# Attention results kept with features on partitions, their norms as rows over DRAM

## The chip, the cores and the metric

One NeuronCore of a Trainium2 chip runs the whole program. The metric is the device time of one execution in microseconds (us); a lower time is better. The engines are TensorE (PE, with its weight loads PEld), VectorE (DVE), ScalarE (ACT), GpSimd (POOL) and SyncE (SP). DMA transfers are issued from the queues of SP, ACT and POOL.

## What is computed

One layer of a hybrid decoder block in float32 on 512 tokens and 1024 features: 16 heads of 64 features, 4 of them MoBA (heads 0 to 3), 6 dilated (heads 4 to 9), 6 FoX (heads 10 to 15). The part that the change touches is what stands between a head's softmax and the output projection:

```python
hn = rms_norm(x, norm_g)
proj = hn @ w_in                      # q, k, v, f_logit, g_fox
...
p = softmax(logits);  o = p @ v       # per head, (tokens, 64)
...
y_moba = rms_norm(to_bsd(o_moba), out_gain[:W_MOBA])
y_fox = rms_norm(to_bsd(o_fox), ...) * sigmoid(g_fox)
y_dil = rms_norm(to_bsd(o_dil), ...)
x = x + concat([y_moba, y_fox, y_dil]) @ w_out
x = x + square(relu(rms_norm(x, mlp_norm) @ w_up)) @ w_down
```

`rms_norm` divides a token's features by the root of their mean square, so each group of heads needs one number per token, and each head's softmax one denominator per token.

## The kernel before

Every float32 product is made of three products of the type fp32r: each operand is split into a high and a low part, and hi·hi, hi·lo and lo·hi are added in PSUM. Weights are split as they stream in: ACT casts the high part (`whi`, L118), DVE subtracts it (`wlo`, L119).

There are three stages. The input projection (`product`, L274) runs over nine chunks of columns (q and k of four heads, then v of four heads, four times, then the FoX gate) and eight blocks of 128 input features. Attention's steps are put between its products by a planner that runs when the program is written: a list `steps`, each with what it needs and a lag after it (`LAG`), a running clock and a price for each step (`COST`), and `attend`, which puts the next eligible step after each triple of products. So PE's order is written out by hand. The other engines' orders come from a scheduler that takes the operations in the order in which it thinks their inputs are there. Each engine runs its own list strictly in order. The output projection follows, in two chunks of columns, each in two parts: part 0 over the MoBA and FoX features that are ready, part 1 over the rest, each part added into the residual by DVE (`out_done`, L748). Then comes the MLP (L876 up, L917 down), which the change leaves alone.

A head's way: `stack_step` transposes q and k and swaps their parts between partitions by DMA (`stk`), and loads the head's bias tile on POOL's queue (`alibi`, L485, for heads 0 to 9; `ck`, L479, rows of a cumulated sum in DRAM copied to 128 partitions, for heads 10 to 15; two buffers each). `s_step` makes four blocks of scores (L516), their maximum (DVE, `mn`, L528) and exponentials (ACT, `p`, L530). `pt_step` transposes p (L543) and splits it (`pth` ACT L549, `ptl` DVE L550). `av_step` (L567) multiplies by v. Its weight is v's high and low parts side by side, so the result `ot` has the 64 features of the one part on partitions 0 to 63 and of the other on 64 to 127; ACT copies it out (`ots`, L572).

`o_step` then adds the two parts: four fp32 transposes on PE (L582) put tokens on partitions, a DVE reduction adds the halves (`osum`, L584), and POOL multiplies by the reciprocal of the denominator into `o_grp` (L591). After a group's last head, `group_norm` squares and adds on ACT (L607), takes the root on DVE (`rsqrt`, L284 to L290) and scales on DVE (L618, or L614 together with the gate for FoX). `y_transpose` (L624) brings features back to partitions for the output projection, split by ACT (L627) and DVE (L628). There are 16 o steps of four transposes, and 32 transposes of y.

PSUM has eight banks: four ("m") for attention and the MLP's first half, four ("acc") for the projections.

Of the kernel before, what the change touches and what calls it, by code (L numbers as in the profile page):

```python
# [156 lines left out]
def hymba_block(ctx: ExitStack, tc: tile.TileContext, a, out):  # L157
# [397 lines left out]
    def av_step(h, half):  # L555
        def f():
# [8 lines left out]
            for j, p in blocks:  # L565
                v = vst[h // 4, j][:, h % 4].rearrange("p a d -> p (a d)")
# [34 lines left out]
    def group_norm(g):  # L601
        o = o_grp[g]
        n = o.shape[2]
        ss = small.tile([P, NT], F32, name="oss")
        for t in range(NT):
            junk = att.tile([P, S], F32, name="ots")[:, :n]
            nc.scalar.activation(junk, o[:, t], AF.Square, accum_out=ss[:, t : t + 1])  # L607
        v = small.tile([P, NT], F32, name="ov")
        r = small.tile([P, NT], F32, name="orr")
        nc.vector.tensor_scalar(v, ss, 1.0 / n, EPS, op0=ALU.mult, op1=ALU.add)  # L610
# [416 lines left out]
```

## Time and profile before

| what | us |
|---|---|
| median of 3 runs | 636.34 (636.05 to 636.53) |
| the profiled execution | 636.59 |
| its span in the trace | 634.8 |
| PE busy | 625.1 (98%) |
| DVE busy | 459.6 (72%) |
| ACT busy | 322.6 (51%) |
| POOL busy | 43.9 (7%) |

PE's busy time is nearly the span, and the granted clock is 0.997 of full speed. Busy time on PE is counted from each matmul's start to its modelled end, and these overlap. What a matmul costs is therefore read from start to start. DVE is busy 72% over the whole, but this mean hides stretches between 124 and 208 us in which it is near 90%.

### The profile page before, as it was taken

The numbers are of one execution on the slowest core, as the hardware profiler recorded it, in microseconds if no ns is written. First come the engines' busy times: TensorE is split into PE (matmuls) and PEld (weight loads), VectorE is DVE, ScalarE is ACT, GpSimd is POOL, SyncE is SP. The second block draws the span as 40 slices with busy tenths as digits, with TensorE's granted clock in tenths as the row PEclk, the third lists the DMA queues.
The fourth block names the chain that finished last, engine by engine and source line by source line (L and its number), as shares of the span: only waits on it lengthen the run. The fifth ranks groups of instructions, "written<-read, shape, count | busy, mean of one in ns | idle before, by whom it ended". The sixth has DMA issues, their size and how long they took to land.

```text
span 634.8 us, 9834 instructions
## 1 busy us (share of the span) xinstructions
PE 625.1 (98%) x3800; PEld 556.0 (88%) x3800; DVE 459.6 (72%) x786; ACT 322.6 (51%) x575; POOL 43.9 (7%) x63
## 2 busy tenths in 40 slices
PE   7999999999999999999999999999999999999997
PEld 6798898898889998888889989898989899989986
DVE  6794695796578666578899766687588766865972
ACT  7457666677777585639553433343334333434320
POOL 4010220121120000001100000000000000000000
PEclk8999999999999999999999999999999999999999
DMA  8534423423522335256624243232530433212213
GB/s 311 160 103 132 125 74 77 131 79 112 138 59 76 101 102 174 74 178 204 133 66 147 71 148 100 83 109 75 167 96 8 163 100 131 68 35 67 68 41 126
DMA packets 24911, 70.03 MB, mean 110 GB/s; under 512 B 3210, under 2 KB 4762, under 8 KB 24864
## 3 DMA queue, kind: packets, MB, share of 16 engines
q1 hardware_dynamic: 18224, 57.84, 28.6%
q10 hardware_dynamic: 4432, 5.77, 3.7%
q0 software_dynamic: 2208, 5.79, 3.7%
q8 instruction: 30, 0.49, 0.3%
q14 instruction: 17, 0.14, 0.1%
HBM read 61.51 MB, written 2.11 MB: 100 GB/s over the span
## 4 chain that ended last, share of the span: by engine, by line
PE 76%; DVE 7%; ACT 1%; issue 1%; DMA 1%; ACTq 0%; POOL 0%; DVEq 0%
PE acc L917 28%; PE m L876 22%; PE acc L274 19%; PE m L516 2%; PE m L567 2%; PE m L543 1%; DVE ptl L550 1%; PE m L497 1%; DMA stk<-stk 1%; DVE qkss L402 1%; DVE wlo L119 1%; DVE qks L420 1%; DVE m L528 1%; DVE qkraw L415 1%; DVE qkv L403 1%
## 5 line engine op out<-in xcount | busy, mean ns | idle before, releaser
L118 ACT CAST whi<-wraw 128x1024 fp32r<-128x1024 f32 (+3 forms) x66 | 66.8, 1015 | 86.5 <-PE acc L917 38.7
L274 PE MATMUL acc<-whi,xh 128*128 128x512 f32 (+3 forms) x284 | 103.5, 364 | 0.7 <-DVE fl L438 0.4
L917 PE MATMUL acc<-hh,whi 128*128 128x512 f32 x256 | 100.2, 391 | 0.0
L917 PE MATMUL acc<-hh,wlo 128*128 128x512 f32 x256 | 99.9, 390 | 0.0
L917 PE MATMUL acc<-hl,whi 128*128 128x512 f32 x256 | 99.6, 389 | 0.0
L119 DVE TENSOR_TENSOR wlo<-wraw,whi 128x1024 fp32r<-128x1024 f32 (+3 forms) x66 | 78.9, 1197 | 28.4 <-ACT whi L118 28.0
L274 PE MATMUL acc<-wlo,xh 128*128 128x512 f32 (+3 forms) x284 | 95.7, 337 | 0.7 <-DVE wlo L119 0.6
L274 PE MATMUL acc<-whi,xl 128*128 128x512 f32 (+3 forms) x284 | 95.8, 337 | 0.0
L876 PE MATMUL m<-zh,whi 128*128 128x256 f32 x224 | 62.8, 280 | 0.0
L876 PE MATMUL m<-zh,wlo 128*128 128x256 f32 x224 | 62.6, 279 | 0.0
L876 PE MATMUL m<-zl,whi 128*128 128x256 f32 x224 | 62.5, 279 | 0.0
L274 PEld LDWEIGHTS acc<-whi,xl 128*128 128x128 f32 x284 | 53.6, 189 | 5.2
L917 PEld LDWEIGHTS acc<-hh,wlo 128*128 128x128 f32 x256 | 48.0, 188 | 10.6 <-DVE wlo L119 0.5
L274 PEld LDWEIGHTS acc<-wlo,xh 128*128 128x128 f32 x284 | 54.0, 190 | 3.7 <-DVE wlo L119 1.5
L274 PEld LDWEIGHTS acc<-whi,xh 128*128 128x128 f32 x284 | 53.7, 189 | 3.7 <-DVE vs L432 0.7
L917 PEld LDWEIGHTS acc<-hl,whi 128*128 128x128 f32 x256 | 48.1, 188 | 9.2 <-issue 0.2
L917 PEld LDWEIGHTS acc<-hh,whi 128*128 128x128 f32 x256 | 48.1, 188 | 9.1 <-issue 0.2
L118 ACT CAST whi<-wsum 128x1024 fp32r<-128x1024 f32 x28 | 29.4, 1049 | 40.2 <-PE m L876 37.6
L926 DVE TENSOR_TENSOR x<-acc,x 128x512 f32<-128x512 f32 (+1 forms) x65 | 42.2, 678 | 9.5 <-PE acc L917 9.4
L119 DVE TENSOR_TENSOR wlo<-wsum,whi 128x1024 fp32r<-128x1024 f32 x28 | 34.3, 1223 | 19.3 <-ACT whi L118 19.3
L530 ACT ACTIVATE p<-m,mn 128x128 f32<-128x128 f32 (+1 forms) x64 | 33.6, 527 | 24.9 <-DVE mn L528 22.8
L876 PEld LDWEIGHTS m<-zh,whi 128*128 128x128 f32 x224 | 42.0, 188 | 1.1
(193 smaller groups left out, 1324.1 us busy)
## 6 DMA issues: line engine op xcount, KB each, us to landing
wraw<-in_w_down SPq DMA_DIRECT2D x32, 512.0 KB, 3.6
ublk<-in_w_up SPq DMA_DIRECT2D x28, 512.0 KB, 3.4
wraw<-in_w_in SPq DMA_DIRECT2D x21, 512.0 KB, 3.8
stk<-stk ACTq DMA_DIRECT2D x32, 128.0 KB, 2.4
wraw<-in_w_out SPq DMA_DIRECT2D x6, 512.0 KB, 4.0
alibi<-in_alibi POOLq DMA_DIRECT2D x10, 256.0 KB, 3.2
x<-in_xT SPq DMA_DIRECT2D x4, 512.0 KB, 5.1
wraw<-in_w_up SPq DMA_DIRECT2D x4, 512.0 KB, 5.4
```

The costliest lines, as they stand in the source:

```text
L118: nc.scalar.copy(hi, raw)
L119: nc.vector.tensor_tensor(lo, raw, hi.bitcast(F32), op=ALU.subtract)
L274: nc.tensor.matmul(dst, lhsT=lhs, rhs=rhs, start=(k == 0 and m == 0), stop=(k == n - 1 and m == 2))
L402: nc.vector.tensor_reduce(ss, sq.rearrange("p (h d) -> p h d", d=DH), axis=AX.X, op=ALU.add)
L403: nc.vector.tensor_scalar(state["v"][:, t], ss, 1.0 / DH, eax[:, t : t + 1], op0=ALU.mult, op1=ALU.add)
L415: nc.vector.tensor_tensor(raw, raw, state["y"][:, t].unsqueeze(2).broadcast_to([P, 8, DH]), op=ALU.mult)
L516: nc.tensor.matmul(ps[:, :n], lhsT=st[0][:, i * P : (i + 1) * P], rhs=st[m][:, :n], start=(m == 1), stop=(m == 2 and h < FOX0),)
L530: nc.scalar.activation(p, ps[:, :n], AF.Exp, bias=mn, scale=-1.0, accum_out=st["den"][:, i : i + 1])
L567: nc.tensor.matmul(ot[:, j * P :], lhsT=v, rhs=p, start=(half == 0 and j == 0), stop=(half == 1 and j == 3))
L876: nc.tensor.matmul(acc[:, f * HALF : (f + 1) * HALF], lhsT=lhs, rhs=rhs, start=first and (f, j, m) == (0, 0, 0), stop=(f, j, m) == (1, 3, ...
L917: nc.tensor.matmul(acc, lhsT=lhs, rhs=rhs, start=(p, k, m) == (0, 0, 0), stop=(p, k, m) == (1, 1, 2))
L926: nc.vector.tensor_tensor(dst[:, cols], acc[:, cols], dst[:, cols], op=ALU.add)
```

## The change

The result of a head stays as `av_step` leaves it, features on partitions. The new code for that is `result`, which takes the place of `o_step`, and `norm_step`, which takes the place of `group_norm`; `y_transpose` becomes `y_parts` without PE.

- The two halves of `ots` are added by a DMA that accumulates, issued on POOL's queue (64 partitions of 2 KB, L617).
- The reciprocal denominators, four columns on 128 partitions, are written to a row in DRAM (`row_to_dram`, 512 pieces of 4 bytes, L351) and read back as 64 copies of that row (`row_copies`, L356), both on POOL's queue. DVE multiplies the sum by the rows (L618). POOL's multiplication L591 goes.
- v's parts are laid out by parity of the head, so that an odd head's sum lands on partitions 64 to 127; its two operations for each tile become four (L450, L451).
- A pair's squares are made by ACT and added by DVE (L628) into a tile that takes a buffer of `ck` (group 0) or of `alibi` (groups 1 and 2). Four matmuls with one column (L636) add them over the partitions; the root goes over DRAM to rows on 128 partitions.
- Groups 0 and 1 are multiplied by these rows (DVE, L650). FoX's are multiplied onto the products: in part 1 of the output projection DVE multiplies each PSUM bank by the row (L785) ahead of the residual's addition (L786).
- The gate chunk of the input projection is turned round: 72 products of 512 columns in place of 96 of 384; DVE multiplies by x's row (in place of ACT's L466), and again into the FoX result (L659).
- The planner's lag "norm" goes from 9 to 10, and the steps "o" and "y" have no price any more.

```diff
+    def row_to_dram(src, name):
+        d = dram.tile([1, S], F32, name=name)
+        nc.gpsimd.dma_start(d.rearrange("o (t p) -> p (o t)", p=P), src)
+        return d
+    def row_copies(dst, d):
+        nc.gpsimd.dma_start(dst, bass.AP(tensor=d.tensor, offset=d.offset, ap=[[0, dst.shape[0]], [1, S]]))
...
+        rows_d["x"] = row_to_dram(rx, "rx_d")
...
-    o_grp = [att.tile([P, NT, (h1 - h0) * DH], F32, name=f"o{g}", bufs=1) for g, (h0, h1, _) in enumerate(GROUPS)]
-    gsig = att.tile([P, NT, NFOX * DH], F32, name="gsig", bufs=1)
+    o_grp = [att.tile([P, (h1 - h0) // 2, S], F32, name=f"o{g}", bufs=1) for g, (h0, h1, _) in enumerate(GROUPS)]
+    gsig = att.tile([P, NFOX // 2, S], F32, name="gsig", bufs=1)
...
+    def gate_operands(k, f, wh, wl):
+        wh, wl = wh[:, f * P : (f + 1) * P], wl[:, f * P : (f + 1) * P]
+        return ((wh, xh[:, k]), (wh, xl[:, k]), (wl, xh[:, k])), lambda acc: acc
...
-            v = att.tile([P, 4, 2, DH], F32R, name="vs", bufs=8)
-            av = acc[:, :256].rearrange("p (h d) -> p h d", d=DH)
-            nc.scalar.activation(v[:, :, 0], av, AF.Copy, scale=rx[:, t : t + 1])
-            nc.vector.scalar_tensor_tensor(
-                v[:, :, 1], av, rx[:, t : t + 1], v[:, :, 0].bitcast(F32),
-                op0=ALU.mult, op1=ALU.subtract,
-            )
+            v = att.tile([P, 2, 4, DH], F32R, name="vs", bufs=8)
+            av = acc[:, :256].rearrange("p (j o d) -> p j o d", o=2, d=DH)
+            for m in range(2):
+                src, hi, lo = av[:, :, m], v[:, :, 3 * m], v[:, :, 1 + m]
+                nc.scalar.activation(hi, src, AF.Copy, scale=rx[:, t : t + 1])
+                nc.vector.scalar_tensor_tensor(
+                    lo, src, rx[:, t : t + 1], hi.bitcast(F32), op0=ALU.mult, op1=ALU.subtract
+                )
...
-    def g_done(t, acc):
-        nc.scalar.activation(gsig[:, t], acc[:, : NFOX * DH], AF.Copy, scale=rx[:, t : t + 1])
+    def g_done():
+        rxb = att.tile([P, S], F32, name="alibi")
+        row_copies(rxb, rows_d["x"])
+        def done(f, acc):
+            nc.vector.tensor_tensor(gsig[:, f], acc, rxb, op=ALU.mult)
...
+            if i == NT - 1:
+                rd = small.tile([P, NT], F32, name="rden")
+                nc.vector.reciprocal(rd, st["den"])
+                d = row_to_dram(rd, f"rd{h}")
+                r0 = DH * (h % 2)
+                st["rden"] = small.tile([P, S], F32, name="rowb")[r0 : r0 + DH]
+                row_copies(st["rden"], d)
...
+                result(h, ot)
...
-    def o_step(h):
...
+    def result(h, ot):
+        g = 0 if h < 4 else 1 if h < 10 else 2
+        k, odd = divmod(h - GROUPS[g][0], 2)
+        sb = att.tile([P, S], F32, name="ots")
+        nc.scalar.copy(sb, ot)
+        main, rest = (sb[DH * m : DH * (m + 1)] for m in (odd, 1 - odd))
+        nc.gpsimd.dma_start(main, rest, accum_op=ALU.add)
+        nc.vector.tensor_tensor(o_grp[g][DH * odd : DH * (odd + 1), k], main, heads[h]["rden"], op=ALU.mult)
+        if odd:
+            o = o_grp[g][:, k]
+            if k == 0:
+                sums[g] = att.tile([P, S], F32, name="alibi" if g else "ck")
+                nc.scalar.activation(sums[g], o, AF.Square)
+            else:
+                sq = att.tile([P, S], F32, name="ots")
+                nc.scalar.activation(sq, o, AF.Square)
+                nc.vector.tensor_tensor(sums[g], sums[g], sq, op=ALU.add)
...
+    def norm_step(g):
         def f():
-            st = heads[h]
             ps = bank("m")
-            for i in range(NT):
-                nc.tensor.transpose(out=ps[:, i * P : (i + 1) * P], in_=st["ots"][:, i * P : (i + 1) * P], identity=ident)
-            s = small.tile([P, NT, DH], F32, name="osum")
-            nc.vector.tensor_reduce(
-                s, ps.rearrange("p (i a d) -> p i d a", a=2, d=DH), axis=AX.X, op=ALU.add
-            )
-            rd = small.tile([P, NT], F32, name="rden")
-            nc.vector.reciprocal(rd, st["den"])
-            g = 0 if h < 4 else 1 if h < 10 else 2
-            c = (h - GROUPS[g][0]) * DH
-            nc.gpsimd.tensor_tensor(
-                o_grp[g][:, :, c : c + DH], s, rd.unsqueeze(2).broadcast_to([P, NT, DH]), op=ALU.mult
-            )
-            if h + 1 == GROUPS[g][1]:
-                group_norm(g)
+            for t in range(NT):
+                nc.tensor.matmul(
+                    ps[:, t : t + 1], lhsT=sums[g][:, t * P : (t + 1) * P], rhs=ones[:, :1], start=True, stop=True
+                )
+            n = (GROUPS[g][1] - GROUPS[g][0]) * DH
+            v = small.tile([P, NT], F32, name="ov")
+            r = small.tile([P, NT], F32, name="orr")
+            nc.vector.tensor_scalar(v, ps[:, :NT], 1.0 / n, EPS, op0=ALU.mult, op1=ALU.add)
+            rsqrt(r, v, NT)
+            rows = small.tile([P, S], F32, name="rowb")
+            row_copies(rows, row_to_dram(r, f"rg{g}"))
+            if g == 2:
+                rows_d["fox"] = rows
+            else:
+                for k in range(n // P):
+                    nc.vector.tensor_tensor(o_grp[g][:, k], o_grp[g][:, k], rows, op=ALU.mult)
+                    if g == 0:
+                        y_parts(0, k)
...
+    def y_parts(g, k):
+        src = o_grp[g][:, k]
+        if g == 2:
+            nc.vector.tensor_tensor(src, src, gsig[:, k], op=ALU.mult)
...
-    LAG = {"qk": 2, "root": 3, "zero": 0.0, "each": 2.5, "v": 2.5, "f": 5, "stack": 5.5, "s": 3.5, "pt": 3, "av": 3, "free": 1, "cum": 7, "norm": 9}
-    COST = {"stack": 0.25, "s": 0.3, "pt": 0.4, "av": 0.6, "o": 0.43, "y": 0.22, "f": 0.43, "root": 0.0, "norm": 0.0, "sig": 0.0}
+    LAG = {"qk": 2, "root": 3, "zero": 0.0, "each": 2.5, "v": 2.5, "f": 5, "stack": 5.5, "s": 3.5, "pt": 3, "av": 3, "free": 1, "cum": 7, "norm": 10}
+    COST = {"stack": 0.25, "s": 0.3, "pt": 0.4, "av": 0.6, "ss": 0.43, "y": 0.0, "f": 0.43, "root": 0.0, "norm": 0.0, "sig": 0.0}
...
+        for g, (h0, h1, _) in enumerate(GROUPS):
+            if h + 1 == h1:
+                step(("ss", g, 0), norm_step(g), [(("av", h, 1), "norm")])
...
+            if part == 1:
+                nc.vector.tensor_tensor(acc, acc, rows_d["fox"], op=ALU.mult)
...
+    attend_until(("ss", 1, 0))
+    for k in range(3):
+        y_parts(1, k)
+        step(("y", 2, k), partial(y_parts, 2, k), [(("av", FOX0 + 2 * k + 1, 1), "zero"), (("sig", 0, 0), "zero")])
...
+    attend_until(("y", 2, 2))
+    attend_until(("ss", 2, 0))
```

Where instructions stand now. POOL, heads 0 to 2 (`rd` is a head's row of reciprocals in DRAM, `rowb` its copies). Before:

```order
L485 DMA alibi_603<-in_alibi 128x512
L485 DMA alibi_870<-in_alibi 128x512
L485 DMA alibi_1229<-in_alibi 128x512
L400 TENSOR_TENSOR qkraw_822<-qkraw_822,kg_817 128x256
L400 TENSOR_TENSOR qkraw_854<-qkraw_854,kg_817 128x256
L591 TENSOR_TENSOR o0_189<-osum_846,rden_848 128x4x64
```

After:

```order
L509 DMA alibi_609<-in_alibi 128x512
L351 DMA rd0_678<-rden_676 128x4x1
L356 DMA rowb_680<-rd0_678 64x512
L509 DMA alibi_886<-in_alibi 128x512
L351 DMA rd1_759<-rden_757 128x4x1
L356 DMA rowb_761<-rd1_759 64x512
L617 DMA ots_798<-ots_798 64x512
L509 DMA alibi_1247<-in_alibi 128x512
L351 DMA rd2_819<-rden_817 128x4x1
L416 TENSOR_TENSOR qkraw_848<-qkraw_848,kg_843 128x256
```

Between the loads of the bias tiles there are now, for each head, a row out, its copies and the addition of the halves, and the multiplication `qkraw` of the next heads' norms stands behind them.

DVE, between the last scores of head 1 and its `ptl` (`kg`, `qkss` and `qkv` belong to the norms of later heads' q and k). Before:

```order
L119 TENSOR_TENSOR wlo_1002<-wraw_703,whi_1001 128x1024
L550 TENSOR_TENSOR ptl0_810<-m_804,pth0_809 128x512
L388 SCALAR_TENSOR_TENSOR kg_817<-qg_816,kg_817 128x256
L402 TENSOR_REDUCE qkss_827<-qksq_823 128x8
L550 TENSOR_TENSOR ptl1_835<-m_830,pth1_834 128x384
L403 TENSOR_SCALAR qkv_821<-qkss_827,eax_186 128x8
L584 TENSOR_REDUCE osum_846<-m_841 128x256
L402 TENSOR_REDUCE qkss_859<-qksq_855 128x8
L550 TENSOR_TENSOR ptl2_867<-m_862,pth2_866 128x384
```

After:

```order
L119 TENSOR_TENSOR wlo_1024<-wraw_715,whi_1023 128x1024
L618 TENSOR_TENSOR o0_185<-ots_798,rowb_680 64x512
L559 RECIPROCAL rden_817<-den_770 128x4
L582 TENSOR_TENSOR ptl0_836<-m_830,pth0_835 128x512
L404 SCALAR_TENSOR_TENSOR kg_843<-qg_842,kg_843 128x256
L418 TENSOR_REDUCE qkss_853<-qksq_849 128x8
L582 TENSOR_TENSOR ptl1_861<-m_856,pth1_860 128x384
L419 TENSOR_SCALAR qkv_847<-qkss_853,eax_182 128x8
L582 TENSOR_TENSOR ptl2_872<-m_867,pth2_871 128x384
```

Head 0's multiplication by its row, L618, stands ahead of head 1's `ptl`; the reduction `osum` L584 stood between the `ptl`.

POOL, about the first FoX heads. Before:

```order
L485 DMA alibi_1969<-in_alibi 128x512
L591 TENSOR_TENSOR o1_190<-osum_1752,rden_1754 128x4x64
L485 DMA alibi_2010<-in_alibi 128x512
L591 TENSOR_TENSOR o1_190<-osum_1868,rden_1870 128x4x64
L463 DMA cum_d_193<-ck_2000 6x512
L479 DMA ck_2048<-cum_d_193 128x512
L591 TENSOR_TENSOR o1_190<-osum_2027,rden_2029 128x4x64
L479 DMA ck_2180<-cum_d_193 128x512
```

After:

```order
L617 DMA ots_1939<-ots_1939 64x512
L481 DMA cum_d_189<-ck_2024 6x512
L503 DMA ck_2027<-cum_d_189 128x512
L503 DMA ck_2297<-cum_d_189 128x512
L509 DMA alibi_1989<-in_alibi 128x512
L351 DMA rd8_2093<-rden_2091 128x4x1
L356 DMA rowb_2095<-rd8_2093 64x512
L351 DMA rd9_2174<-rden_2172 128x4x1
L356 DMA rowb_2176<-rd9_2174 64x512
L617 DMA ots_2215<-ots_2215 64x512
```

The bias tile of head 9 (`alibi_1989`; `alibi_2010` before) now stands behind the cumulated sum's way over DRAM; one of the two `alibi` buffers holds group 1's squares there.

## Rows read from the trace of the kernel before

**Rows 1.** Page, parts 1 and 4: busy time and chain by engine.

```profile
PE 625.1 (98%) x3800; PEld 556.0 (88%) x3800; DVE 459.6 (72%) x786; ACT 322.6 (51%) x575; POOL 43.9 (7%) x63
...
PE 76%; DVE 7%; ACT 1%; issue 1%; DMA 1%; ACTq 0%; POOL 0%; DVEq 0%
```

**Rows 2.** Waits of PE: us in total, times, longest.

```profile
PE acc L274 <- DVE wlo L119: 0.6, 1, 0.6
PE m L567 <- DVE ptl L550: 0.6, 1, 0.6
```

**Rows 3.** Windows: length, then busy us and instructions of each engine, clock.

```profile
124.00:148.00 24.00, 24.00 (x175) 22.59 (x174) 20.29 (x51) 17.12 (x38) 5.90 (x8) 1.00 0.34 105
...
178.00:208.00 30.00, 29.49 (x212) 27.39 (x210) 26.50 (x72) 22.94 (x56) 5.67 (x8) 1.00 0.26 72
```

**Rows 4.** Timeline of PE about an o step: start, us, instruction.

```profile
127.73 0.60 PE L582 MATMUL m<-ident,ots 128*128 128x128 f32 x4
...
128.86 0.49 PE L543 MATMUL m<-ident,p 128*128 128x128 f32 x3
```

**Rows 5.** Chain in order of time: start, us, what.

```profile
264.22 9.63 PE acc L274 x42
273.85 0.98 PE m L624 x9
```

**Rows 6.** PE's groups of instructions by line and form: busy, mean ns.

```profile
L354 PE MATMUL m<-ones,qksq 128*128 128x1 f32 x16 | 1.8, 245 | 0.0
```

**Rows 7.** DVE's groups by line and form.

```profile
L584 DVE TENSOR_REDUCE osum<-m 128x256 f32<-128x512 f32 x16 | 10.9, 684 | 6.3 <-PE m L582 6.3
...
L748 DVE TENSOR_TENSOR x<-acc,x 128x512 f32<-128x512 f32 x16 | 10.5, 684 | 0.3 <-PE acc L274 0.3
...
L432 DVE SCALAR_TENSOR_TENSOR vs<-acc,rx,vs 128x256 fp32r<-128x256 f32 x16 | 7.2, 478 | 0.0
...
L614 DVE SCALAR_TENSOR_TENSOR o<-o,orr,gsig 128x384 f32<-128x384 f32 x4 | 2.2, 615 | 0.1
```

**Rows 8.** ACT's groups by line and form.

```profile
L572 ACT COPY ots<-m 128x512 f32<-128x512 f32 x16 | 9.4, 587 | 11.3 <-PE m L567 11.2
```

**Rows 9.** POOL's groups by line and form: a DMA row gives the issue alone.

```profile
L760 POOL DMA_DIRECT2D v<-sq x3 | 2.7, 894 | 32.8 <-ACT zh L751 22.5 <-DMA v<-sq 5.7 <-ACT whi L118 4.5
```

**Rows 10.** DMA issues: queue, count, KB each, median us to landing (`v` accumulates).

```profile
stk<-stk ACTq DMA_DIRECT2D x32, 128.0 KB, 2.4
...
ck<-cum_d POOLq DMA_DIRECT2D x6, 256.0 KB, 3.7
...
v<-sq POOLq DMA_DIRECT2D x3, 256.0 KB, 4.9
...
cum_d<-ck POOLq DMA_DIRECT2D x1, 12.0 KB, 2.9
```

**Rows 11.** Timeline of POOL, two bias tiles and the cumulated sum; in brackets the idle time before.

```profile
65.43 0.55 POOL L485 DMA_DIRECT2D alibi<-in_alibi  x1 [5.50 <-DVE mn L528]
71.41 0.54 POOL L485 DMA_DIRECT2D alibi<-in_alibi  x1 [5.43 <-DVE mn L528]
...
161.12 0.54 POOL L463 DMA_DIRECT2D cum_d<-ck  x1 [9.13 <-DVE ck L462]
164.34 0.58 POOL L479 DMA_DIRECT2D ck<-cum_d  x1 [2.68 <-DMA cum_d<-ck]
```

**Rows 12.** Timeline of PE, head 1's last scores and its product with `ptl`.

```profile
68.48 0.56 PE L516 MATMUL m<-stk,stk 128*128 128x384 f32 x2
...
78.41 0.81 PE L567 MATMUL m<-ptl,vs 128*128 128x512 f32 x4
```

**Rows 13.** Timeline of DVE between these two.

```profile
71.43 1.23 DVE L119 TENSOR_TENSOR wlo<-wraw,whi 128x1024 fp32r<-128x1024 f32 x1 [0.32 <-ACT whi L118]
72.59 0.69 DVE L550 TENSOR_TENSOR ptl<-m,pth 128x512 fp32r<-128x512 f32 x1
...
75.91 0.55 DVE L550 TENSOR_TENSOR ptl<-m,pth 128x384 fp32r<-128x384 f32 x1
```

More of the change, by code (lines that the diff above doesn't have):

```diff
@@ L293, in hymba_block @@
     p1 = ExitStack()
-    p1.enter_context(tc.tile_pool(name="edgex", bufs=1)).tile([P, 64], F32, name="edgex")
     xpool = p1.enter_context(tc.tile_pool(name="xpool", bufs=1))
@@ L463, in cumulate @@
         nc.gpsimd.dma_start(cum_d, cum)
-    def g_done(t, acc):
-        nc.scalar.activation(gsig[:, t], acc[:, : NFOX * DH], AF.Copy, scale=rx[:, t : t + 1])
+    def g_done():
[3 more added lines that the diff above has]
+            nc.vector.tensor_tensor(gsig[:, f], acc, rxb, op=ALU.mult)
+        return done
     def gate():
@@ L565, in f @@
             for j, p in blocks:
[L566 removed]
+                v = vst[h // 4, j][:, h % 4 // 2, 2 * (h % 2) : 2 * (h % 2) + 2].rearrange("p a d -> p (a d)")
                 nc.tensor.matmul(
@@ L597, in o_step @@
         return f
     yT = {0: [att.tile([P, 2, S], F32R, name=f"y0{m}", bufs=1) for m in "hl"]}
[L601 to L610, printed above, removed]
-        rsqrt(r, v, NT)
-        for t in range(NT):
+    sums = {}
@@ new lines, in norm_step, with f @@
+    def norm_step(g):
+        def f():
+            ps = bank("m")
+            for t in range(NT):
[9 more added lines that the diff above has]
+            row_copies(rows, row_to_dram(r, f"rg{g}"))
@@ L613, in group_norm @@
             if g == 2:
-                nc.vector.scalar_tensor_tensor(
-                    o[:, t], o[:, t], r[:, t : t + 1], gsig[:, t], op0=ALU.mult, op1=ALU.mult
-                )
-            else:
-                nc.vector.tensor_scalar(o[:, t], o[:, t], r[:, t : t + 1], None, op0=ALU.mult)
-    def y_transpose(g, t):
-        n = o_grp[g].shape[2] // P
-        ps = bank("m")
-        for k in range(n):
-            nc.tensor.transpose(out=ps[:, k * P : (k + 1) * P], in_=o_grp[g][:, t, k * P : (k + 1) * P], identity=ident)
-        src = ps[:, : n * P].rearrange("p (k q) -> p k q", q=P)
-        hi, lo = (y[:, :, t * P : (t + 1) * P] for y in yT[g])
+                rows_d["fox"] = rows
+            else:
+                for k in range(n // P):
+                    nc.vector.tensor_tensor(o_grp[g][:, k], o_grp[g][:, k], rows, op=ALU.mult)
+                    if g == 0:
+                        y_parts(0, k)
@@ L627, in y_transpose @@
+        return f
+    def y_parts(g, k):
+        src = o_grp[g][:, k]
+        if g == 2:
+            nc.vector.tensor_tensor(src, src, gsig[:, k], op=ALU.mult)
+        hi, lo = (y[:, k] for y in yT[g])
         nc.scalar.copy(hi, src)
         nc.vector.tensor_tensor(lo, src, hi.bitcast(F32), op=ALU.subtract)
-    LAG = {"qk": 2, "root": 3, "zero": 0.0, "each": 2.5, "v": 2.5, "f": 5, "stack": 5.5, "s": 3.5, "pt": 3, "av": 3, "free": 1, "cum": 7, "norm": 9}
-    COST = {"stack": 0.25, "s": 0.3, "pt": 0.4, "av": 0.6, "o": 0.43, "y": 0.22, "f": 0.43, "root": 0.0, "norm": 0.0, "sig": 0.0}
+    LAG = {"qk": 2, "root": 3, "zero": 0.0, "each": 2.5, "v": 2.5, "f": 5, "stack": 5.5, "s": 3.5, "pt": 3, "av": 3, "free": 1, "cum": 7, "norm": 10}
@@ L662, in hymba_block @@
             step(("av", h, half), av_step(h, half), needs)
-        step(("o", h, 0), o_step(h), [(("av", h, 1), "av"), (("o", h - 1, 0), "free")])
-        if h + 1 == GROUPS[0][1]:
-            for t in range(NT):
-                step(("y", 0, t), partial(y_transpose, 0, t), [(("o", h, 0), "norm")])
+        for g, (h0, h1, _) in enumerate(GROUPS):
+            if h + 1 == h1:
+                step(("ss", g, 0), norm_step(g), [(("av", h, 1), "norm")])
         if h == 15:
@@ L710, in hymba_block @@
     for c, (kind, i) in enumerate(IN_CHUNKS):
-        done = {"g": lambda i: g_done, "qk": lambda i: qk_parts[i][0], "v": v_done}[kind](i)
+        done = {"g": lambda i: g_done(), "qk": lambda i: qk_parts[i][0], "v": v_done}[kind](i)
         n = a[f"w_in{c}"].shape[2]
-        for _ in product(in_first[c], list(range(NK)), in_operands(n), NT, done):
+        gates = kind == "g"
+        n, count, operands = (S, NFOX // 2, gate_operands) if gates else (n, NT, in_operands(n))
+        for _ in product(in_first[c], list(range(NK)), operands, count, done):
             tokens += 1
@@ L762, in out_done @@
         return done
-    attend_until(("o", GROUPS[1][1] - 1, 0))
-    for g, at in ((2, len(steps)), (1, 0)):
-        for t in range(NT):
-            step(("y", g, t), partial(y_transpose, g, t), [(("o", GROUPS[g][1] - 1, 0), "norm")])
-            steps.insert(at + t, steps.pop())
-    attend_until(("y", 1, NT - 1))
+    attend_until(("ss", 1, 0))
+    for k in range(3):
+        y_parts(1, k)
+        step(("y", 2, k), partial(y_parts, 2, k), [(("av", FOX0 + 2 * k + 1, 1), "zero"), (("sig", 0, 0), "zero")])
     for c, part, ks in OUT_ORDER[:2]:
```

8 lines of the change are left out of this document (1 added, 7 removed).

## The prediction

> **What bounds the kernel now.** The page first: PE is busy 98% of the span, and PE's own work makes up 76% of the chain that ended last [rows 1]. The list of PE's waits comes next: for weights (`wlo`) and for attention's split parts (`ptl`) it waited only once each, 0.6 us [rows 2]. So PE's work sets the end, and a slot taken off PE should come back in full. The windows qualify that. In two stretches of the input projection, where the norms of the next heads' q and k are made beside the scores, DVE is busy 85% (20.29 of 24.00) and 88% (26.50 of 30.00) [rows 3], and PE follows just behind it. In such a stretch what PE saves gains nothing, and what holds DVE is paid by PE. The forecast weighs the one against the other.
>
> **PE's share.** An o step occupies PE for 1.13 us together with three products [rows 4]. A product of 512 columns costs 9.63 / 42 = 0.229 [rows 5], so the four transposes cost 1.13 − 0.69 = 0.44, and sixteen of them 7.0. Nine transposes of y take 0.98, so 0.109 each [rows 5]. 32 of them make 3.5, and 10.5 with the o steps. Added are three norm steps of four one-column matmuls. The statistics of x have 8 such matmuls in the code and 16 rows in the trace, 1.8 us busy [rows 6], so twelve are 24 rows, at about a transpose's slot 2.6 (end below: 1.3, if only half of a row's time counts). The gate turned round is 72 × 0.229 = 16.5 us; 96 products of 384 columns were 16.9 at 0.176, which is 0.229 scaled by columns with its fixed part. Sum: −10.5 + 2.6 − 0.4 = −8.3. If nothing waited, the profiled execution's 636.59 would become 628.3.
>
> **DVE's share.** L618 (512 columns, 64 partitions) takes the place of the reduction L584 at about the same 0.684 [rows 7]. Added: the squares' additions, 5 × 0.684 = 3.4; rows on group results, 5 × 0.684 = 3.4; the gate's two passes, 6 × 0.684 = 4.1; FoX's row on the products, 8 × 0.684 = 5.5; v in halves, 32 shorter operations for 16 of 0.478, between 0 and 7.6, taken as 2.3 since halves keep the fixed part. Gone: L614, 2.2 [rows 7], and at most as much for the scaling of the other groups. Net about +14 us, of which some 0.6 us lies in each group of four heads where DVE paces PE; the rest lies beside PE's work. ACT loses as much as it gains.
>
> **What is new on the path: DVE waits for a transfer.** Before, DVE's `osum` waited for PE. Now L618 waits for ACT's copy (0.59 [rows 8]), an accumulating DMA from POOL's queue (issue 0.89 [rows 9]) and its landing. That landing is not in the trace. Below it is bounded by a plain swap of the same 128 KB, 2.4, and above by an accumulate of twice the bytes, 4.9 [rows 10]; I take 3.7, the middle. Since DVE runs in order, everything behind L618 is held: `wlo`, `ptl` and q's and k's norms.
>
> Head 0 shows it. Call T the end of its product with v: in the order of after it stands right ahead of head 1's block of scores of 384 columns, at 68.48 in the trace [rows 12]. Ahead of L618 DVE has the `wlo`, done at 72.66 [rows 13], T + 4.2. The accumulate goes out about T + 1.5 and lands at T + 5.2: DVE stands for 1.0. Behind L618 (0.6 from start to start) stand a reciprocal, three `ptl`, `kg`, `qkss`, `qkv`. Before, the row from the first `ptl` to the end of the third took 3.9 (72.59 to 76.46 [rows 13]) with the reduction and a second `qkss` in it; without these two, 2.85. So the last `ptl` is done at T + 8.65. PE asked for it 9.9 after T (78.41 [rows 12]); without the o step (0.44) and one triple of products (0.69) that the new order puts elsewhere, at T + 8.8. A reserve of 2 us is used up by one head, with the middle landing; with 4.9 PE waits 1.
>
> POOL's queue decides the rest. For each head it now issues the bias tile (0.55 [rows 11]), a row of reciprocals, its copies, and the accumulate (0.89). The copies wait until the row has landed: the one such passage in the trace, the cumulated sum, left POOL standing 2.68 [rows 11], with a landing of 2.9 [rows 10]. That is 0.55 × 3 + 0.89 + 2.7 = 5.2 us for each head, while heads come as close as 6 us (two bias tiles at 65.43 and 71.41 [rows 11]), and q's and k's multiplication stands in that queue too.
>
> I count the holds in the same way for each group of four heads, with the extra DVE work, less what reserve was there:
> - heads 0 to 3: holds 1.4 (head 0's 1.0, 0.4 later) + 0.6 − 1.0 = +1.0;
> - heads 4 to 7: group 0's norm row goes out and returns over DRAM (2.9 + 3.7 behind two issues) with DVE's L650 waiting, half of it covered, 0.75; heads 4 and 5 0.5 each; + 0.6 = +2.3;
> - heads 8 to 11: one `alibi` buffer holds squares, and head 9's bias tile stands behind the cumulated sum's passage in the queue, 1.0; head 8's row behind that, 2.1; head 9's, 1.0; + 0.6 − 0.1 = +4.6;
> - heads 12 to 15: +1.8, two late holds and the FoX gate's passes;
> - output projection: FoX's row (issues and landings, 0.55 + 2.9 + 0.55 + 3.7 = 7.7 after the root) lands about when the first bank of part 1 is full, and each bank then needs two DVE operations: +1.2.
> Sum +10.9. Outside the paced stretches PE keeps its saving: four o steps 1.8, the transposes of y1 and y2 24 × 0.109 = 2.6, the gate 0.4, less one norm step 0.9: −3.9. Net +7.0: 636.59 + 7.0 = 643.6, or 643.3 from the median of 636.34. By the landing's two ends (3.7 ± 1.3 in some seven heads that hold, two thirds of it paid) it is 637.5 to 650.
>
> **Rivals.**
> A, the transfers are hidden and PE stays the bound. Mechanism: the orders were made with the transfers' time in mind, and where L618 stands, other work has filled DVE until the row lands. For it: PE waited almost nowhere before [rows 2], and head 0's count still closes with 0.15 to spare. Against it: 85 and 88% DVE [rows 3] and POOL's 5.2 us for each head. The price is then PE's share alone, 628.3; with a third of the holds left, 632. It decides when the accumulate lands by about T + 4.2, that is a landing of 2.7. The Trainium skill's page "DMA: Bandwidth & Descriptors", section "Anatomy of one DMA — SWDGE (gpsimd) path", fits a transfer from this queue as 2.0 us and bytes at 436 GB/s: an estimate of 2.3 us for 128 KB, and of 2.6 for 256 KB. This trace's accumulates of 256 KB took 4.9, so it does not agree for this kind; by the page's figure nothing is held and A holds.
>
> B, the queue falls behind. A row out is 512 pieces of four bytes, and the trace has no such transfer. If it takes 5 us in place of 2.9, a head needs 7.3 us of POOL's queue against 6 between close heads, and about 1 us for each of a dozen heads is added to the forecast: 655. The same page's "Specifications" say that pieces under 512 bytes are read, modified and written; no run here shows what that costs.
>
> C, the two cancel: holds of about a third less than counted, and PE's saving kept in heads 0 to 7 as well: 636.
>
> **How the numbers follow.** Forecast 0.50 (643, its own range 637.5 to 650), A 0.30, B 0.14, C 0.06. Two executions of this kernel can be told apart from about 0.2% on (1.3 us). Faster is A, 0.30; same is C, 0.06; slower the forecast and B, 0.64. The range goes from A's price, 628, to 653, short of B's, and leaves out most of B and a little of A's low end.
>
> **What would show it.** In the trace of after, DVE should wait on `ots` (L618) for 5 to 15 us in all, and PE on `wlo`, `ptl` or `qks` for more than the 0.6 of now. POOL's copies (L356) should wait some 2.7 us each time for their row, and the landing of the accumulate should read 3 to 4.5. PE's busy time should fall by about 8. The forecast falls if PE's waits stay under 2 us in all (then A), and is too low if the landing of `rd` reads 5 us or the qk multiplications on POOL start late (then B).

## The result, and the profile after

The changed kernel takes 778.37 us (777.07 to 780.07), before 636.34: the ratio is 1.2229, with an interval of 1.2213 to 1.2245. It is 142 us slower. The forecast was slower, 643, with a range that ended at 653; the size is off by a factor of twenty (142 us against 7). All times and ratios here are of fast executions; one slow one, of e3 (657.9), is left out.

The page of after, busy times, granted clock and the chain (the answers to [rows 1]):

```profile
PE 645.8 (83%) x3704; PEld 564.6 (73%) x3704; DVE 472.5 (61%) x810; ACT 323.4 (42%) x567; POOL 73.4 (9%) x103
...
PEclk9999689968988798867896999999999999999999
...
PE 46%; issue 6%; DMA 4%; DVE 1%; POOL 1%; ACT 0%; DVEq 0%; POOLq 0%
```

PE is no longer fed: 83% in place of 98%. Of the 142 us by which the span grows (776.6 in place of 634.8), 121 are PE standing (130.8 in place of 9.7) and 21 are PE busy for longer. Nearly all of the loss lies ahead of the MLP's products at L876 (L913 in after). They start at 456.9 in place of 316.5, and from there the kernels take the same time within 1.5 us. From the chains of before and of after:

```profile
316.48 5.65 PE m L876 x48
```

```profile
456.90 5.58 PE m L913 x48
```

PE's busy time did not fall by 8 us, it rose by 21, because the granted clock falls where PE stands. Windows of after, of the late heads with the output projection and of the rest (columns as in [rows 3]):

```profile
300.00:430.00 130.00, 79.54 (x362) 66.34 (x361) 56.62 (x120) 46.83 (x95) 13.44 (x20) 0.79 0.53 105
430.00:776.00 346.00, 341.31 (x2054) 302.61 (x2053) 256.66 (x303) 132.91 (x164) 4.13 (x5) 1.00 0.31 94
```

A granted share of 0.79 is a mixture of the two levels, 1.2 and 2.4 GHz, in a stretch in which PE works 80 of 130 us. A single wait shows the order. At 104.98 PE has stood 5.57 us for a swap (`stk`). In the 3.3 us after that the clock is at the lower level and PE gets through 15 instructions; then it is at the upper level, and in 3.3 us there are 27:

```profile
104.98:108.30 3.32, 3.32 (x15) 3.32 (x16) 1.61 (x6) 1.47 (x5) 0.00 (x0) 0.50 0.08 21
108.70:112.00 3.30, 3.30 (x27) 3.17 (x26) 2.88 (x11) 1.26 (x3) 0.00 (x0) 1.00 0.07 16
```

The clock thus added to the loss, but only after PE had begun to stand.

The list of waits of after, the longest, and those of PE (answers to [rows 2]):

```profile
POOL rowb L356 <- DMA rd<-rden: 112.0, 13, 9.7
DVE o L618 <- DMA ots<-ots: 99.0, 13, 18.8
...
PE m L521 <- DVE ptl L582: 49.0, 4, 17.6
PE acc L274 <- DVE x L786: 18.7, 3, 12.4
PE m L540 <- DMA stk<-stk: 18.6, 3, 12.0
```

The order of events is to be read from the top. POOL stands 112 us for the rows that it has just sent to DRAM (13 waits, 8.6 each; the prediction put 2.7). Behind them in its queue go the accumulates, and DVE stands 99 us for these. Behind DVE's multiplication stand `ptl` and the rest, and PE stands for `ptl`. The DMA list of after (answers to [rows 10]) has the transfer that begins it:

```profile
wraw<-in_w_in SPq DMA_DIRECT2D x21, 512.0 KB, 6.9
...
rowb<-rd POOLq DMA_DIRECT2D x16, 128.0 KB, 4.4
ots<-ots POOLq DMA_DIRECT2D x16, 128.0 KB, 4.4
...
rd<-rden POOLq DMA_DIRECT2D x16, 2.0 KB, 9.6
```

Two kilobytes, written in 512 pieces of four bytes, land after 9.6 us; a bias tile of 256 KB took 3.2 before, and the weights of the input projection, which have nothing to do with the rows, went from 3.8 to 6.9.

The worked case of the prediction, head 0, shows it whole. Timeline of POOL of after, with the idle time before each instruction:

```profile
63.00 0.76 POOL L351 DMA_DIRECT2D rd<-rden  x1 [0.57 <-DVE rden L559]
72.90 0.53 POOL L356 DMA_DIRECT2D rowb<-rd  x1 [9.14 <-DMA rd<-rden]
73.42 0.57 POOL L509 DMA_DIRECT2D alibi<-in_alibi  x1
73.98 0.77 POOL L351 DMA_DIRECT2D rd<-rden  x1
84.35 0.53 POOL L356 DMA_DIRECT2D rowb<-rd  x1 [9.60 <-DMA rd<-rden]
84.87 0.93 POOL L617 DMA_DIRECT2D ots<-ots  x1
```

and of DVE:

```profile
88.72 0.68 DVE L618 TENSOR_TENSOR o<-ots,rowb 64x512 f32<-64x512 f32 x1 [13.49 <-DMA ots<-ots]
```

T, the end of head 0's product with v, is 71.2. DVE is ready for L618 at 88.72 − 13.49 = 75.2, so T + 4.0 (the prediction: T + 4.2). But the accumulate goes out at T + 13.7 (the prediction: T + 1.5), because head 1's row with its wait of 9.6 stands ahead of it, and DVE goes on at T + 17.5 (the prediction: T + 5.2).

### The profile page after: what moved, and what is told of

Same layout as the page of the kernel before. It is cut to its first block, busy times and chain, and to the rows that moved or that the text cites. A ratio compares the mean times of both kernels' runs of the same rounds, so it can differ in the third digit from the quotient of the medians.

```text
span 776.6 us, 9758 instructions
## 1 busy us (share of the span) xinstructions
PE 645.8 (83%) x3704; PEld 564.6 (73%) x3704; DVE 472.5 (61%) x810; ACT 323.4 (42%) x567; POOL 73.4 (9%) x103
## 4 chain that ended last, share of the span: by engine, by line
PE 46%; issue 6%; DMA 4%; DVE 1%; POOL 1%; ACT 0%; DVEq 0%; POOLq 0%
PE acc L954 23%; PE m L913 18%; PE acc L274 5%; DMA wraw<-in_w_up 1%; DMA rd<-rden 1%; DMA rowb<-rg 1%; DMA ots<-ots 0%; DVE x L786 0%; POOL ots L617 0%; PE m L866 0%; POOL rowb L356 0%; DVE acc L785 0%; ACT t5h L859 0%; POOL rd L351 0%; DVE wlo L123 0%
## 5 line engine op out<-in xcount | busy, mean ns | idle before, releaser
L274 PE MATMUL acc<-whi,xh 128*128 128x512 f32 (+2 forms) x252 | 94.2, 374 | 4.6 <-DVE vs L451 3.1
L274 PE MATMUL acc<-wlo,xh 128*128 128x512 f32 (+2 forms) x252 | 88.4, 351 | 0.0
L274 PE MATMUL acc<-whi,xl 128*128 128x512 f32 (+2 forms) x252 | 88.3, 350 | 0.0
L618 DVE TENSOR_TENSOR o<-ots,rowb 64x512 f32<-64x512 f32 x16 | 11.7, 733 | 99.0 <-DMA ots<-ots 99.0
L913 PE MATMUL m<-zh,wlo 128*128 128x256 f32 x224 | 63.3, 282 | 0.0
L913 PE MATMUL m<-zl,whi 128*128 128x256 f32 x224 | 63.1, 282 | 0.0
L913 PE MATMUL m<-zh,whi 128*128 128x256 f32 x224 | 63.0, 281 | 0.0
L540 PE MATMUL m<-stk,stk 128*128 128x128 f32 (+3 forms) x128 | 32.9, 345 | 28.4 <-DMA stk<-stk 18.6
L274 PEld LDWEIGHTS acc<-whi,xh 128*128 128x128 f32 x252 | 50.1, 199 | 8.6 <-issue 5.5
L521 PE MATMUL m<-identr,qks 128*128 128x128 f32 x128 | 15.5, 259 | 49.0 <-DVE ptl L582 49.0
L274 PEld LDWEIGHTS acc<-whi,xl 128*128 128x128 f32 x252 | 50.0, 198 | 6.0
L521 PEld LDWEIGHTS m<-identr,qks 128*128 128x128 f32 x128 | 14.4, 149 | 52.6 <-DVE ptl L582 49.9
L274 PEld LDWEIGHTS acc<-wlo,xh 128*128 128x128 f32 x252 | 50.4, 200 | 3.1 <-DVE wlo L119 0.2
```

The lines of the kernel that those rows point to most:

```text
L274: nc.tensor.matmul(dst, lhsT=lhs, rhs=rhs, start=(k == 0 and m == 0), stop=(k == n - 1 and m == 2))
L521: nc.tensor.transpose(out=ps[:, t * P : (t + 1) * P].bitcast(F32R), in_=src, identity=identr)
L540: nc.tensor.matmul(ps[:, :n], lhsT=st[0][:, i * P : (i + 1) * P], rhs=st[m][:, :n], start=(m == 1), stop=(m == 2 and h < FOX0),)
L618: nc.vector.tensor_tensor(o_grp[g][DH * odd : DH * (odd + 1), k], main, heads[h]["rden"], op=ALU.mult)
L913: nc.tensor.matmul(acc[:, f * HALF : (f + 1) * HALF], lhsT=lhs, rhs=rhs, start=first and (f, j, m) == (0, 0, 0), stop=(f, j, m) == (1, 3, ...
```

## The experiments

Times are medians beside runs of the kernel before on the same chip (636.1 to 636.6 there). The theory (1) was that the row in four-byte pieces makes nearly all of the loss, the rival that the accumulates do.

| kernel | us | ratio to before, interval |
|---|---|---|
| after | 778.4 | 1.2229 (1.2213 to 1.2245) |
| e13 multiplication by the rows on POOL | 787.4 | 1.2371 (1.2331 to 1.2412) |
| e11 rows and copies on SP's queue | 738.3 | 1.1602 (1.1584 to 1.1620) |
| e10 rows written, nobody waits for them | 730.1 | 1.1503 (1.1460 to 1.1546) |
| e4 rows turned on PE, four pieces | 714.6 | 1.1227 (1.1203 to 1.1251) |
| e12 as e10, halves not added | 701.4 | 1.1005 (1.0952 to 1.1058) |
| e5 as e4, turned at a better place | 674.5 | 1.0595 (1.0574 to 1.0615) |
| e7 as e5, v split as in before | 669.4 | 1.0515 (1.0500 to 1.0531) |
| e1 no row written but that of x | 652.9 | 1.0253 (1.0235 to 1.0271) |
| e2 as e1, halves not added | 647.9 | 1.0179 (1.0117 to 1.0242) |
| e9 no new transfer but the row of x | 638.6 | 1.0028 (1.0013 to 1.0043) |
| e3 before, rows written from POOL, unread | 653.5 | 1.0240 (1.0180 to 1.0300) |
| e6 before, rows written from ACT, unread | 650.6 | 1.0209 (1.0185 to 1.0232) |
| e8 other ways for halves and denominators | 649.2 | 1.0220 (1.0189 to 1.0250) |
| e8 with a longer lag | 654.3 | 1.0277 (1.0255 to 1.0298) |

### e1 and e2: without the rows, and without the sum

```diff
     def row_to_dram(src, name):
+        if rows_d:
+            return rows_d["x"]
```

> After, but the rows of reciprocals (16) and of norms (3) are not written to DRAM; every copy reads the row of x instead, so denominators and norms are left out of the result. Copies, accumulating transfers and all of DVE's and PE's work stay. Theory 1 (the write of a row in 512 pieces of four bytes, 9.8 us to landing, on POOL's queue makes nearly all of the +142 us): the time falls to the count made before without it, about 643 (635 to 655). Rival (the accumulating transfer that DVE waits for makes it, 99 us of DVE's waits): it stays above 700.

```diff
-        nc.gpsimd.dma_start(main, rest, accum_op=ALU.add)
```

> As e1, and the halves are not added either: DVE multiplies ACT's copy directly. What is left is PE's saving and the other work of DVE. Theory 1: only some 5 to 15 us below e1, near 630. Rival: the large fall comes here, not in e1.

e1 takes 652.9: without the rows' writes 125 of the 142 us are gone, although every copy, every accumulate and all the work of DVE are still there. e2 is 5 us lower still, but its executions spread from 643.5 to 652.3, so the 5 us are not clear of noise, and the 630 that I expected are far off. The rival of e1 falls as it was put: accumulates are not by themselves what DVE stands for. In e1 they land in 2.8 us, and the rows that DVE needs in 3.4:

```profile
rowb<-rx_d POOLq DMA_DIRECT2D x16, 128.0 KB, 3.4
ots<-ots POOLq DMA_DIRECT2D x16, 128.0 KB, 2.8
```

The prediction took 3.7 for this accumulate. The Trainium skill's page "DMA: Bandwidth & Descriptors" ("Anatomy of one DMA — SWDGE (gpsimd) path") gives, by its fit, an estimate of 2.3; 2.8 is nearer to it than to the middle that I took. The accumulates of 256 KB landed in 3.3 and 3.4 here, against 4.9 and 4.5 before, so the 4.9 had been a loose upper bound.

### e3 and e6: the rows alone

The kernel before, with the 16 rows also written and never read; e3 from POOL's queue, e6 from ACT's.

```diff
             nc.vector.reciprocal(rd, st["den"])
+            d = dram.tile([1, S], F32, name=f"rd{h}")
+            nc.gpsimd.dma_start(d.rearrange("o (t p) -> p (o t)", p=P), rd)
```

> The kernel before with the 16 rows of reciprocals also written to DRAM from POOL's queue, and nobody reads them. It measures the disputed transfer by itself. Theory 1: its landing is 9 to 10 us here too, although nothing stands behind it, and the time stays at 636 (within 1 us). Rival (the write is slow only because copies and accumulates crowd its queue): the landing is 2 to 4 us.

> As e3 (before, 16 rows written in four-byte pieces, nobody reads them), but issued from ACT's queue instead of POOL's. e3 showed 18 us although nobody waits for the row: the other transfers' landings grew (the stk swaps from 2.4 to 3.7 us). Theory 2 (the pieces keep the shared DMA engines busy, whichever queue they come from): 645 to 665, landing near 10 us, stk above 3 us. Rival (it is POOL's queue): within 2 us of 636.

For e3 I expected no change of time, and that was wrong: by the ratios it is 15 us slower (11 to 19), and e6 is 13 us slower, as expected there. The transfer itself takes about the same as in after, whichever queue sends it. DMA list of e3:

```profile
wraw<-in_w_in SPq DMA_DIRECT2D x21, 512.0 KB, 6.7
stk<-stk ACTq DMA_DIRECT2D x32, 128.0 KB, 3.7
alibi<-in_alibi POOLq DMA_DIRECT2D x10, 256.0 KB, 6.2
...
rd<-rden POOLq DMA_DIRECT2D x16, 2.0 KB, 10.4
```

and of e6:

```profile
rd<-rden ACTq DMA_DIRECT2D x16, 2.0 KB, 10.6
```

So a row costs twice: by its own 10 us, and by what it does to every other transfer that runs beside it, from all three queues (the swaps `stk` from 2.4 to 3.7, bias tiles from 3.2 to 6.2, weights from 3.8 to 6.7). In e3 PE's longest wait is then a swap, with 6.5 us in all, where it was 0.3 before. In that execution, 10 us longer than before, PE stands 7 us longer (16.5 in place of 9.7) and is busy for 3.5 us longer, since the clock falls here too. The window behind one of these waits (2.16 us, until 87.55):

```profile
87.55:92.00 4.45, 4.45 (x19) 4.35 (x20) 2.37 (x10) 1.20 (x5) 0.00 (x0) 0.50 0.78 52
```

The Trainium skill's "DMA: Bandwidth & Descriptors" ("Specifications") gives 512 bytes as the least for a transfer at full rate; below that the DMA engine reads, changes and writes. The runs agree that such pieces are slow; that they slow the others too is what the runs add.

### e4, e5 and e7: the row in four pieces

PE turns the 128x4 reciprocals into 4x128, ACT copies them out, and the write has 4 pieces of 512 bytes. In e4 the turn stands behind the other reads of its PSUM bank, in e5 ahead of them.

```diff
+                nc.tensor.transpose(out=ps[:NT, 384:512], in_=st["rd"], identity=ident)
...
+        nc.scalar.copy(t, ps)
+        d = dram.tile([1, S], F32, name=name)
+        nc.gpsimd.dma_start(d.rearrange("o (t p) -> (o t) p", p=P), t)
```

> After, with each row turned by one transpose on PE (128x4 to 4x128), copied by ACT, and written in 4 pieces of 512 bytes; copies and accumulates as in after. Theory 1: the row lands in 2 to 3 us, POOL stands about 2 us for each copy, and the time is 640 to 655. Rival (any passage over DRAM with the copy behind it stalls the queue): above 700.

> As e4, but PE turns the row of reciprocals before the bank's other columns are read, not after. In e4 PE stood 51 us for DVE's ptl at that transpose, by where it was put. Theory 1 (the four-byte row was the loss; in 4 pieces it lands in 1.6 us and disturbs nobody): the time is that of e1, 645 to 660. Rival (the passage over DRAM with a copy waiting for it on POOL's queue costs by itself): 680 or more.

The row now lands in 1.6 us, and the accumulates and copies in 3. DMA list of e5:

```profile
rowb<-rd POOLq DMA_DIRECT2D x16, 128.0 KB, 2.9
ots<-ots POOLq DMA_DIRECT2D x16, 128.0 KB, 3.2
...
rd<-rowb POOLq DMA_DIRECT2D x16, 2.0 KB, 1.6
```

e4 missed its range all the same: its 714.6 is a time that the rival had named, but it comes from a fault of mine. PE waited 51.3 us at the turn itself.

```profile
PE m L356 <- DVE ptl L587: 51.3, 16, 6.8
```

The row of the waits names it: the turn writes into other columns of the bank that DVE's `ptl` was still reading. e5 has it ahead of that, and takes 674.5, so 104 us below after, with the same numbers computed. It lies between the range that I gave (645 to 660) and that of the rival (680 or more). POOL still stands 20 us for the rows and 66 for ACT's small copies ahead of them, with accumulates and q's and k's multiplications behind. Whether this is the reason isn't shown: PE's own waits are 35 us in all (18 in e1), the longest 5.9, and e5 has 19 turns and copies that e1 doesn't have.

```profile
POOL rd L360 <- ACT rowb L358: 66.0, 13, 9.6
...
POOL rowb L365 <- DMA rd<-rowb: 20.1, 11, 3.0
```

e7 takes v's split back to one operation of each engine for a tile:

```diff
-            for m in range(2):
-                src, hi, lo = av[:, :, m], v[:, :, 3 * m], v[:, :, 1 + m]
+            nc.scalar.activation(v[:, :, 0], av, AF.Copy, scale=rx[:, t : t + 1])
```

> As e5, with v split as in before: one operation of ACT and one of DVE for a tile of 256 columns, each head's high part first. The sum of the halves is the same. In e1 PE stood 4.4 us for v's DVE operation (L451). Expected: 3 to 6 us below e5; a rival that v's halves are hidden gives no difference.

It is 5.2 us faster than e5, as expected. These 5.2 are both engines' second operations together. The halves are summed in the end whichever comes first, so the layout by parity wasn't needed.

### e9: the change without its transfers

```diff
+                if "rows" not in rows_d:
+                    rows_d["rows"] = small.tile([P, S], F32, name="rowb", bufs=1)
+                    row_copies(rows_d["rows"], d)
+                st["rden"] = rows_d["rows"][r0 : r0 + DH]
-                row_copies(st["rden"], d)
```

> After without any of its new transfers: no rows written, one row copied once and used for all denominators and norms, the halves not added, v split as in before. Denominators, norms and the addition of the halves are left out. What remains is the change's saving on PE and its other DVE work. The prediction's rival A gave 628.3 for this. If the count of PE's slots holds: 627 to 632. Rival (DVE's added work, 14 us, is on the path in the dense stretches as the prediction's forecast says): 634 to 640.

638.6, which is 2 us above before and 10 above the count of PE's slots, so on the rival's side (634 to 640). The saving is there, and it is given back. The seventh chunk of columns starts 0.65 us earlier, in the timelines of PE of before and of e9:

```profile
150.33 0.47 PE L274 MATMUL acc<-whi,xh 128*128 128x512 f32 x1 [0.40 <-DVE fl L438]
```

```profile
149.68 0.44 PE L274 MATMUL acc<-whi,xh 128*128 128x512 f32 x1
```

By then e9 has also done head 7's product with v and ten transposes of p that come later in before, some 2 us of PE's time by their spacing. That is a lead of about 3 us, and the prices of the prediction give 3.1 there (seven o steps and eight transposes of y, less one norm step: 3.1 + 0.9 − 0.9). At the first product of the MLP 0.4 is left of the 8.3:

```profile
294.09 0.40 PE L274 MATMUL acc<-zh,whi 128*128 128x512 f32 x1
```

```profile
293.71 0.47 PE L274 MATMUL acc<-zh,whi 128*128 128x512 f32 x1 [1.40 <-ACT whi L118]
```

Waits of PE in e9:

```profile
PE m L577 <- ACT p L554: 2.4, 1, 2.4
...
PE m L540 <- DMA stk<-stk: 1.7, 2, 1.0
PE acc L274 <- ACT whi L118: 1.4, 1, 1.4
...
PE acc L274 <- DVE x L786: 1.0, 2, 0.5
```

The longest, of 2.4 us, lies in the seventh chunk (until 170.06), among heads 8 to 11, where the forecast had put its largest loss; the last row is the output projection's, where each bank needs two DVE operations. Behind the longest the clock falls:

```profile
170.06:173.80 3.74, 3.74 (x12) 3.00 (x13) 3.23 (x7) 2.29 (x7) 0.00 (x0) 0.54 0.30 75
```

Of the 10 us, 6 are PE standing (15.4 in place of 9.7), and by estimate 1.6 are the clock (0.96 granted over the 40.75 us of that chunk). 1.4 lie in the MLP, which the change leaves alone: from its first product at L913 to the end it takes 319.9, in before 318.5. The reason for these 1.4, and the last 1 to 2 us, stay open.

### e10 to e13: how the rows' 125 us divide

e10 keeps all row writes of after and lets every copy read the row of x; e12 takes the accumulate out as well.

```diff
     def row_copies(dst, d):
+        d = rows_d["x"]
```

> After with all its row writes, but every copy reads the row of x, so nobody waits for a row that was just written (denominators and norms are left out of the result). It divides the rows' 125 us (after 778, e1 653) into what the pieces do to the other transfers and what the waiting for them costs. Theory 2 (waiting on POOL's queue is the larger part; the pieces disturb the others by some 15 to 30 us, as in e3 and e6): 665 to 690. Rival (the disturbance is the larger part): above 720.

> As e10 (rows written in four-byte pieces, nobody waits for them), and the halves are not added (left out of the result): DVE waits for no accumulate. Without the writes this is e2, 648. Theory 3 (the accumulate lands late behind the pieces and DVE, in order, stands for it with ptl behind): 660 to 675, 12 to 27 above e2 as the writes cost in the kernel before. Rival (weights, swaps and bias tiles late): 700 or more.

Both went against my expectation and are in the range of the rival. Taken away first, the waiting for a row costs 48 us (778.4 to 730.1), and then what the pieces do to other transfers costs 77 (730.1 to 652.9), the larger part. The other order was not run, and it may divide the 125 us otherwise: in after, where POOL stands for each row, less goes out beside one than in e10 (`stk` lands in 2.4 there and 3.5 in e10, `ots` in 4.4 and 6.3). Of the DMA list of e10, the accumulates, which land in 2.8 without the writes, and of its waits, DVE's:

```profile
ots<-ots POOLq DMA_DIRECT2D x16, 128.0 KB, 6.3
```

```profile
DVE o L619 <- DMA ots<-ots: 50.6, 11, 9.1
```

Without any accumulate (e12, 701.4 against e2's 647.9) the pieces still cost 53. PE then stands for another transfer, the swaps, which land in 6.7 in place of 2.4:

```profile
PE m L541 <- DMA stk<-stk: 38.5, 6, 11.8
```

```profile
stk<-stk ACTq DMA_DIRECT2D x32, 128.0 KB, 6.7
```

PE waits up to 12 us for a swap, about as long as a row takes. It is a matter of which transfer goes out while a row is on its way. The trace of e12 has the landing of 24 swaps: the 12 that were in flight together with a row took 8.8 to 15.5 us, the 12 others 2.2 to 4.6. Of all of them, least, median and most:

```profile
DMA to landing us min/median/max: 2.2/6.7/15.5
```

In e3 the order of work is another, and the same rows cost 15.

e11 issues rows and copies from SP's queue; e13 has POOL multiply by the rows, so that DVE doesn't stand for the accumulate.

```diff
-        nc.gpsimd.dma_start(d.rearrange("o (t p) -> p (o t)", p=P), src)
+        nc.sync.dma_start(d.rearrange("o (t p) -> p (o t)", p=P), src)
```

> After with the rows and their copies issued from SP's queue, so that POOL stands for no row; SP's queue, which loads the weights, stands instead. If POOL's standing (131 us; accumulates, bias tiles and the q and k multiplications behind it) is what costs: 680 to 720, unless the weights come late. If it is the row's own way (9.8 and 4.4 us to landing) that DVE waits for whatever queue it is on: 750 or more.

```diff
-        nc.vector.tensor_tensor(o_grp[g][DH * odd : DH * (odd + 1), k], main, heads[h]["rden"], op=ALU.mult)
+        nc.gpsimd.tensor_tensor(o_grp[g][DH * odd : DH * (odd + 1), k], main, heads[h]["rden"], op=ALU.mult)
```

> After with the multiplication by the rows (L618) on POOL instead of DVE, all transfers as in after. DVE then stands for no head's accumulate or row; POOL does, with the next head's row behind it. Theory 3: clearly below after (778), 690 to 740, and DVE's waits on transfers gone but for the norms. Rival (what counts is POOL's queue): as after or slower.

e11 gains 40 us, between its two expectations: POOL stands for no row any more, and the pieces disturb as before (`ots` 6.0, `stk` 5.8 us to landing). e13 gains nothing (787.4, 9 us above after). Moving the wait off DVE moves it elsewhere: PE now waits for the exponentials, because ACT, whose squares wait for POOL's multiplication, stands.

```profile
ACT ots L627 <- POOL o L618: 66.6, 5, 26.1
...
PE m L540 <- ACT p L554: 43.4, 4, 16.6
```

So the theory that DVE's standing in order is the mechanism falls in this form. On POOL too the work behind the late transfer is late.

### e8: another way to the same layout

No transfer for the heads: POOL multiplies the exponentials by the reciprocals while tokens are on partitions, ACT copies one half over to the other's partitions, DVE adds from PSUM; the four norm rows are turned on PE. v is as in before, and the planner's lags are adapted.

```diff
+            for j in which:
+                q = st["p"][j]
+                nc.gpsimd.tensor_scalar(q, q, st["rd"][:, j : j + 1], None, op0=ALU.mult)
...
+        nc.scalar.copy(sb[main], ot[rest])
+        nc.vector.tensor_tensor(o_grp[g][main, k], ot[main], sb[main], op=ALU.add)
```

> Features stay on partitions as in after, but without transfers for the heads: POOL multiplies the exponentials by the reciprocals while tokens are on partitions, ACT copies one half of the result onto the other half's partitions and DVE adds them from PSUM; v as in before; the rows of x and of the three norms are turned on PE and written in 4 pieces. If the transfers were the loss and PE's saving is real, this should fall below before: 628 to 637. Rival (POOL's multiplication, about 3.6 us for each head, delays the transposes of p instead): 645 or more.

> As e8, with the planner's lag from a head's scores to its transposes raised from 5 to 7 (after: 3.5), which gives POOL's multiplication more time. If e8 waits on POOL, this is faster than e8 by what PE waited there; if not, equal or 1 to 3 us slower.

649.2 and 654.3: 20 us better than the best version with the transfers, e7, but 2% slower than before. That is not the 628 to 637 that I expected, but a time that the rival had named (645 or more). Still, PE waits only 0.4 us for POOL itself, and the longer lag, which gives POOL more time, makes it 5 us slower. PE's largest wait is at a turned norm row, which waits for DVE's root (3.4 us in two waits); the others are of about 2 us and less. What e8 loses stays open. No version of mine beats the kernel before.

## Why the prediction was wrong, point by point

- **The landing of the row** is the first step that failed. The trace of before showed no transfer of 512 four-byte pieces, and the text says so under rival B. But the sum took 2.9 for it, from the cumulated sum of 12 KB [rows 10], which goes out in six pieces of 2 KB, and 5 at most, from no row. It took 9.6 us. The accumulate's landing, which was bounded from both sides, came out inside its bounds where no row was written (2.8), and its median in after, 4.4, does too. The list of before had one more small transfer, `gains`, 12 KB onto 128 partitions, 5.1 us. It would hardly have been a better bound, since at the same time `ident`, 64 KB, took 5.0.
- **What a transfer does to others** is the second step that failed: the sum has no term for it. The prediction counted each transfer by its own landing. e10 against e1 shows 77 us, and e12 against e2 53, from pieces that nobody waits for.
- **The forecast's sum without the row.** In e1, which writes no row for a head, the time is 652.9, 9 us above the 643.6 of the sum. So the other terms are too small as well. e1 is 14 us above e9, for accumulates, copies and v's halves together; the sum's holds are about 7 of its 11 us. e5, whose row lands in 1.6, sooner than the 2.9 of the sum, is at 674.5 with its turns and copies.
- **Rival B** had a part of the mechanism, POOL's queue falling behind, but the price of the row was half of what it is. So it stood at 655.
- **POOL's queue as the place** was right: the copies wait 8.6 us each, where 2.7 was expected, and the order of head 0's instructions on POOL and DVE was as read from the order of after. DVE was ready at T + 4.0, as counted.
- **PE's share**, −8.3, is real as far as head 7 (in e9 a lead of about 3 us, as by its prices), and is lost again from the later heads to the MLP's first product (0.4 left), in the main as the forecast said and rival A denied. Rival A's 628 isn't reached even without any of the new transfers.
- **DVE's added work**: v's halves were priced at 2.3 us of DVE's time and cost 5.2 on the path, ACT's part included (e5 to e7).
- Of the signs named at the end of the prediction, DVE's wait on `ots` was 99.0 in place of 5 to 15, the accumulate's landing 4.4 was in its range, and PE's busy time rose. The sign that the forecast is too low, a landing of `rd` of 5 us, was there with 9.6.

## What to carry to other kernels

Price a DMA by its pieces before its bytes: turn a column that has to become a row on the chip first, so that it goes out in a few long pieces. Ask of each new transfer not only who waits for it, but also which transfers run beside it, and which engine's ordered work stands behind those. Where no row of the trace has a price, a guess of its upper end is no bound, and the range has to stay open on that side. And a short wait of PE can cost more than itself, by the clock behind it.

## What the runs showed that I had not expected

- 512 pieces of 4 bytes to DRAM: 9.6 us from POOL's queue in after, and in the kernel before 10.4 from POOL's and 10.6 from ACT's; 4 pieces of 512 bytes: 1.6 us.
- Sixteen such rows, read by nobody, cost the kernel before 13 to 15 us, through transfers of all three queues and the clock behind PE's waits.
- A wait that is moved to another engine (e13) may keep its price; moved to another queue (e11), it left more than two thirds of the loss. Taking the cause away (e5) gave 104 us.
